# Masked softmax in one pass: 16 pieces of 64 bytes of the output are written early, GpSimd shares the lengths and fills later

## The chip, the cores and the metric

One core of one Trainium2 chip. Times are microseconds (us) of device time for one execution. The spans in the profile are some 2 us shorter than these times (155.5 against 157.49 in the same execution). Where a run was timed in rounds, "ratio" is the mean time of one kernel's fast runs over the mean of the other kernel's fast runs of the same rounds, so it is not quite the ratio of the medians quoted. Single times are used here only for differences of a microsecond or more.

## The reference

`x` is 16 x 8 x 256 x 256 fp32, and `lengths` gives one length between 128 and 255 for each batch.

```python
result = np.zeros_like(x)
for b in range(batch):
    length = lengths[b]
    masked = x[b, :, :, :length].copy()
    masked = masked - np.max(masked, axis=-1, keepdims=True)
    exp_masked = np.exp(masked)
    result[b, :, :, :length] = exp_masked / np.sum(exp_masked, axis=-1, keepdims=True)
```

## The kernel before

A batch is 2.1 MB: 128 partitions of 16 rows of 256 numbers, in one of eight slots of SBUF, the core's on-chip memory (HBM is the large memory that holds `x` and the output). SyncE loads the first four batches and issues every store, on one queue. GpSimd loads the other twelve, each only as wide as its length needs, after filling the unread right-hand columns of four slots once with zeros. VectorE masks, ScalarE takes exponentials with row sums, VectorE multiplies by the inverse sums.

```python
for h in range(2):
    s = slice(h * half, (h + 1) * half)
    nc.sync.dma_start(out=xt[:, 0, s], in_=x_f[0, :, s]).then_inc(s_ld[h], 16)
nc.scalar.dma_start(out=word64, in_=lengths[None, :]).then_inc(s_word, 16)
for b in range(1, ahead):                       # ahead = 4
    nc.sync.dma_start(out=xt[:, b], in_=x_f[b]).then_inc(s_ld[b + 1], 16)
for b in range(batch):
    s_b = s_st[b % 2]
    for s in parts(b):                          # halves and quarters of a batch
        nc.sync.wait_ge(s_out, 2 * b + (s.stop - 1) // half + 1)
        if b >= 2 and s.start == 0:
            nc.sync.wait_ge(s_b, 64 * (b // 2 + 1))
        nc.sync.dma_start(out=out_f[b, :, s, :], in_=xt[:, b % slots, s, :]).then_inc(...)
# ... cut ...
nc.gpsimd.dma_start(out=word64_p, in_=lengths[None, :]).then_inc(s_word_p, 16)
# ... two tiny memsets ...
nc.gpsimd.wait_ge(s_v, 1)
for b in range(ahead, slots):
    nc.gpsimd.memset(xt[:, b, :, low:], 0.0).then_inc(s_fill, 1)
nc.gpsimd.wait_ge(s_word_p, 16)
nc.gpsimd.wait_ge(s_fill, slots - ahead)
nc.gpsimd.wait_ge(s_ld[ahead - 1], 16)          # batch 2 has landed
# ... a loop of GpSimd's twelve loads, each with the width its length picks ...

# VectorE: the bounds
nc.vector.wait_ge(s_word, 16)
nc.vector.tensor_copy(out=len_b, in_=word[:, ::2]).then_inc(s_lenb, 1)
nc.vector.wait_ge(s_lenf, 1)                    # TensorE spreads them over the partitions
step(nc.vector.tensor_scalar(out=len_s, in0=len_f, scalar1=big, scalar2=None, op0=ALU.mult))
```

The softmax here doesn't subtract the row's maximum and nothing guards it: scores larger than these inputs give would overflow.

## Time and profile before

| | before |
|---|---|
| time, median of 3 | 157.06 us (156.95 to 157.23) |
| span of the profile | 155.5 us |
| VectorE, ScalarE, GpSimd busy | 77%, 68%, 12% |
| bytes moved | 62.08 MB (28.51 read from HBM, 33.55 written) |

A profile of a kernel like this is read from the rows of the DMA engines first. If they are full from end to end, the time is bytes over rate (here 62.08 MB at a mean of 399 GB/s, 155.6 us, for a span of 155.5), and the question for any change is whether it alters the bytes, the rate, or the idle ends. The prediction below shows those rows. In the timeline, columns are start, duration, engine, line, operation, "out<-in", count, and in brackets how long the engine stood idle before and what ended that. This is GpSimd at the top of the kernel before:

```profile
1.83 0.64 POOL L146 DMA_DIRECT2D word_p<-in_lengths_dram  x1
2.47 0.12 POOL L148 MEMSET seed<- 1x1 f32 x2
2.54 5.33 POOL L151 MEMSET xt<- 128x1536 f32 x4
```

It is busy from 1.83 to 7.87 without a gap. And the view of waits says how long VectorE stood before its masks for a load (total, times, longest):

```profile
DVE xt L197 <- DMA xt<-in_x_dram: 10.2, 6, 2.4
```

### The profile page before, as it was taken

Reading aid. Unit: us, or ns where it says so; the run is one execution under the profiler, and the core shown is the slowest. Engines: PE = TensorE matmul, PEld = TensorE weight load, DVE = VectorE, ACT = ScalarE, POOL = GpSimd, SP = SyncE. Lnnn points to the kernel's source line nnn. Section 1 sums busy time; section 2 is a strip of 40 time slices with the busy share of each in tenths; the row PEclk is TensorE's granted clock in tenths of the full one; section 3 lists DMA queues with packets and bytes.
Section 4 is the critical chain, followed back from the end, with each engine's and each line's share of the span. In section 5 each row is a group of like instructions: output and inputs, shape, how many; then the busy total and the mean of one; then the engine's idle time right before and its main releaser. Section 6 shows DMA issues by size and latency. Waiting matters only on the chain.

```text
span 155.5 us, 1320 instructions
## 1 busy us (share of the span) xinstructions
PE 0.2 (0%) x1; PEld 0.1 (0%) x1; DVE 120.0 (77%) x84; ACT 105.1 (68%) x514; POOL 19.4 (12%) x26
## 2 busy tenths in 40 slices
PE   0000000000000000000000000000000000000000
PEld 0000000000000000000000000000000000000000
DVE  4963999999999968939895999997977999920000
ACT  3029599999989893956969298989592989400000
POOL 7900031003020202002020202020100000000000
DMA  4999999999999999999999999999999999999991
GB/s 116 428 443 426 434 312 388 416 442 427 393 395 410 415 416 406 420 410 413 409 412 419 402 417 406 415 411 405 425 421 432 420 419 432 457 426 422 415 434 61
DMA packets 10452, 62.08 MB, mean 399 GB/s; under 512 B 930, under 2 KB 1026, under 8 KB 7122
## 3 DMA queue, kind: packets, MB, share of 16 engines
q1 hardware_dynamic: 6336, 41.95, 65.9%
q0 software_dynamic: 4112, 20.12, 32.0%
q14 instruction: 2, 0.02, 0.0%
q10 hardware_dynamic: 2, 0.00, 0.0%
HBM read 28.51 MB, written 33.55 MB: 399 GB/s over the span
## 4 chain that ended last, share of the span: by engine, by line
DMA 67%; DVE 11%; issue 6%; POOLq 2%; SPq 1%; POOL 0%; DVEq 0%
DMA xt<-in_x_dram 60%; DVE xt L224 7%; DMA out_dram<-xt 7%; DVE xt L197 3%; POOLq L100 1%; POOLq L136 1%; POOLq L131 1%; SPq L109 1%; DVE inv_sum L221 0%; POOL xt L131 0%; SPq L112 0%; POOLq L159 0%; POOLq L155 0%; DVEq L214 0%; POOLq L161 0%
## 5 line engine op out<-in xcount | busy, mean ns | idle before, releaser
L251 ACT ACTIVATE xt<-xt x256 | 102.4, 402 | 27.2 <-DVE xt L197 27.2
L224 DVE TENSOR_TENSOR xt<-xt,inv_sum 128x2048 f32<-128x2048 f32 x32 | 73.3, 2292 | 1.1
L251 ACT ACTIVATION_READ_ACCUMULATOR xt<-xt x256 | 48.2, 188 | 0.0
L197 DVE SCALAR_TENSOR_TENSOR xt<-down,len_s,xt 128x2048 f32<-128x2048 f32 (+1 forms) x17 | 37.7, 2222 | 11.1 <-DMA xt<-in_x_dram 10.2
L131 POOL DMA_DIRECT2D xt<-in_x_dram x12 | 12.7, 1057 | 89.7 <-issue 45.7
L221 DVE RECIPROCAL inv_sum<-row_sum 128x8 f32<-128x8 f32 x32 | 6.2, 195 | 2.4 <-ACT xt L251 2.4
L185 DVE CAST len_b<-word 1x16 bf16<-1x16 int32 x1 | 5.6, 5595 | 0.4 <-DMA word<-in_lengths_dram 0.4
L151 POOL MEMSET xt<- 128x1536 f32 x4 | 5.3, 1392 | 0.0
L243 ACT ACT_TABLE_LOAD x1 | 1.3, 1283 | 1.6 <-SPq L79 1.6
L180 DVE TENSOR_SCALAR down<-iota_i 128x256 f32<-128x256 int32 x1 | 0.3, 295 | 1.6 <-POOL iota_i L142 1.6
L146 POOL DMA_DIRECT2D word_p<-in_lengths_dram x1 | 0.6, 643 | 0.1
L188 DVE TENSOR_SCALAR len_s<-len_f 128x16 f32<-128x16 f32 x1 | 0.2, 174 | 0.4 <-PE len_f L167 0.4
L142 POOL IOTA iota_i<- 128x256 int32 x1 | 0.3, 331 | 0.6 <-SPq L79 0.6
L243 ACT ACTIVATE warm<-const-float32-0.0 128x1 f32<-128x1 f32 x1 | 0.2, 203 | 0.0
L145 POOL MEMSET ones<- 1x128 bf16 x1 | 0.2, 194 | 0.0
L167 PE MATMUL len_f<-len_b,ones 1*128 1x16 bf16 x1 | 0.2, 168 | 8.0 <-DVE len_b L185 8.0
L269 POOL MEMSET const-float32-0.0<- 128x1 f32 x1 | 0.1, 98 | 0.3 <-issue 0.3
L148 POOL MEMSET seed<- 1x1 f32 x2 | 0.1, 88 | 0.0
L167 PEld LDWEIGHTS len_f<-len_b,ones 1*128 1x128 bf16 x1 | 0.1, 98 | 8.0 <-issue 8.0
L269 POOL MEMSET const-float32-1.0<- 128x1 f32 x1 | 0.1, 98 | 0.0
L269 POOL MEMSET const-bfloat16-1.0<- 128x1 bf16 x1 | 0.1, 98 | 0.0
L269 POOL MEMSET const-uint8-127<- 128x1 uint8 x1 | 0.1, 98 | 0.0
(1 smaller groups left out, 0.0 us busy)
## 6 DMA issues: line engine op xcount, KB each, us to landing
out_dram<-xt SPq DMA_DIRECT2D x16, 1024.0 KB
out_dram<-xt SPq DMA_DIRECT2D x20, 512.0 KB
xt<-in_x_dram SPq DMA_DIRECT2D x3, 2048.0 KB, 16.0
out_dram<-xt SPq DMA_DIRECT2D x3, 2048.0 KB
xt<-in_x_dram POOLq DMA_DIRECT2D x3, 1728.0 KB, 15.9
xt<-in_x_dram POOLq DMA_DIRECT2D x2, 2048.0 KB, 16.0
xt<-in_x_dram POOLq DMA_DIRECT2D x2, 1600.0 KB, 14.5
xt<-in_x_dram POOLq DMA_DIRECT2D x2, 1280.0 KB, 13.6
```

Source lines behind the costliest of these rows:

```text
L100: return nc.values_load(at, engines=[engine], skip_runtime_bounds_check_because="compared with constants, never an address",)
L109: nc.sync.dma_start(out=xt[:, 0, s], in_=x_f[0, :, s]).then_inc(s_ld[h], 16)
L131: nc.gpsimd.dma_start(out=xt[:, slot, :, :w], in_=x_n[:, n, :, :w]).then_inc(s_sw[par], 16)
L136: with nc.gpsimd.If(v <= ws[m]):
L146: nc.gpsimd.dma_start(out=word64_p, in_=lengths[None, :]).then_inc(s_word_p, 16)
L151: nc.gpsimd.memset(xt[:, b, :, low:], 0.0).then_inc(s_fill, 1)
L185: nc.vector.tensor_copy(out=len_b, in_=word[:, ::2]).then_inc(s_lenb, 1)
L197: return nc.vector.scalar_tensor_tensor(out=t, in0=down[:, None, lo:hi].to_broadcast([P, s.stop - s.start, hi - lo]), scalar=len_s[:, b : ...
L221: step(nc.vector.reciprocal(out=inv_sum[:, b, s], in_=row_sum[:, b, s]))
L224: nc.vector.tensor_tensor(out=t, in0=t, in1=inv_sum[:, b, s, None].to_broadcast([P, half, seq_k]), op=ALU.mult,).then_inc(s_out, 1)
L243: nc.scalar.activation(out=warm, in_=nc.const_aps.tensor(0.0, (P, 1), F32), func=EXP)
L251: ins = nc.scalar.activation(out=e, in_=e, func=EXP, accum_out=sum_h[:, bass.ds(i, 1), j])
```

## The change

Two intents. First, the rate falls for some microseconds where the first store comes; if that is an engine's first write to the output, 16 pieces of 64 bytes, meant as one for each engine, written at the top might pay for it early (the true values are stored over them later). Second, VectorE's small cast takes 5.59 us beside GpSimd's early work and ends at 7.89, just after the last of its four fills (7.87; 1.39 each), so GpSimd drops its own copy of the lengths and fills only once the bounds exist.

```diff
-    word64_p = pool.tile([1, batch], mybir.dt.int64, name="word64_p")
-    word_p = word64_p.bitcast(I32)
+    few = 16
+    touch = pool.tile([few, few], F32, name="touch")
@@ before the loads
+        nc.scalar.dma_start(out=word64, in_=lengths[None, :]).then_inc(s_word, 16)
+        out_e = out_f[0].rearrange("(e r) t k -> e r t k", e=few)[:, 0, 0, :few]
+        nc.vector.memset(touch, 0.0).then_inc(s_zero, 1)
+        nc.scalar.wait_ge(s_zero, 1)
+        nc.scalar.dma_start(out=out_e, in_=touch).then_inc(s_touch, 16)
@@ ahead of the stores
+        nc.sync.wait_ge(s_touch, 16)
@@ GpSimd
-        nc.gpsimd.dma_start(out=word64_p, in_=lengths[None, :]).then_inc(s_word_p, 16)
-        nc.gpsimd.wait_ge(s_v, 1)
+        nc.gpsimd.wait_ge(s_v, 2)
...
-        nc.gpsimd.wait_ge(s_word_p, 16)
+        nc.gpsimd.wait_ge(s_word, 16)
...
-                v_len = length(POOL, word_p[0:1, bass.ds(2 * n, 1)])
+                v_len = length(POOL, word[0:1, bass.ds(2 * n, 1)])
```

(The declarations of the semaphores and the line of the lengths in its old place are cut.)

More of the change, by code (lines that the diff above doesn't have):

```diff
@@ L81 @@
         s_word = sem("s_word")
-        s_word_p = sem("s_word_p")
         s_ones = sem("s_ones")
+        s_touch = sem("s_touch")
+        s_zero = sem("s_zero")
         s_lenb = sem("s_lenb")
@@ L109 @@
             nc.sync.dma_start(out=xt[:, 0, s], in_=x_f[0, :, s]).then_inc(s_ld[h], 16)
-        nc.scalar.dma_start(out=word64, in_=lengths[None, :]).then_inc(s_word, 16)
         for b in range(1, ahead):
             nc.sync.dma_start(out=xt[:, b], in_=x_f[b]).then_inc(s_ld[b + 1], 16)
+        nc.sync.wait_ge(s_touch, 16)
         for b in range(batch):
```

## The prediction

> **What bounds the kernel now.** I read the page's busy table and slices first. VectorE is busy 77% of the 155.5 us span and ScalarE 68%, but the row of the DMA engines is full from the second slice to the last but one. In the slices below, each cell is 155.5/40 = 3.9 us; the first row is the mean busy share of the 16 DMA engines in tenths, the second what they moved.
>
> ```profile
> DMA  4999999999999999999999999999999999999991
> GB/s 116 428 443 426 434 312 388 416 442 427 393 395 410 415 416 406 420 410 413 409 412 419 402 417 406 415 411 405 425 421 432 420 419 432 457 426 422 415 434 61
> DMA packets 10452, 62.08 MB, mean 399 GB/s; under 512 B 930, under 2 KB 1026, under 8 KB 7122
> ```
>
> The reader is to see three things: the engines never rest, the bytes are fixed (62.08 MB), and one slice in the middle of full busyness is slow: the sixth, 312 GB/s, with 388 after it. So I cut the span at the stages that the timeline showed (loads of the first four batches alone; the odd stretch; loads and stores mixed; stores alone) in the table of windows. Its last two columns are the DMA share and GB/s.
>
> ```profile
> 1.50:4.00 2.50, 0.00 (x0) 0.00 (x0) 1.99 (x2) 1.49 (x2) 2.40 (x7) 1.00 0.70 197
> 4.00:20.50 16.50, 0.17 (x1) 0.10 (x1) 12.81 (x9) 7.78 (x39) 3.87 (x3) 1.00 1.01 431
> 20.50:24.00 3.50, 0.00 (x0) 0.00 (x0) 3.47 (x4) 3.50 (x19) 1.71 (x2) 1.00 0.97 283
> 24.00:26.00 2.00, 0.00 (x0) 0.00 (x0) 2.00 (x1) 2.00 (x12) 0.03 (x1) 1.00 0.99 412
> 26.00:47.50 21.50, 0.00 (x0) 0.00 (x0) 21.30 (x17) 21.04 (x107) 2.33 (x2) 1.00 1.02 415
> 47.50:123.70 76.20, 0.00 (x0) 0.00 (x0) 65.33 (x48) 59.65 (x295) 8.61 (x8) 1.00 1.02 414
> 123.70:152.30 28.60, 0.00 (x0) 0.00 (x0) 13.15 (x10) 9.64 (x48) 0.00 (x0) 1.00 1.00 426
> ```
>
> Loads alone run at 431, stores alone at 426, the mixture at 414. Only two stretches fall short: the first 2.5 us, and 20.5 to 24, where the share is 0.97 and yet only 283 GB/s move: the packets themselves are slow. At the rate of stores alone the loss is (426 - 283) x 3.5 = 0.50 MB, over 426 GB/s = **1.17 us**. The DMA view of 20.5 to 22.5 says whose packets these are:
>
> ```profile
> DMA packets 32, 0.52 MB, mean 262 GB/s; under 512 B 0, under 2 KB 0, under 8 KB 0
> q1 hardware_dynamic: 32, 0.52, 105.3%
> ```
>
> 32 packets of 16 KB, two per engine, at 1.053 x 2.0 us x 16 / 32 = 1.05 us each, where 16 KB at 431/16 GB/s take 0.61. All lie in the queue of SyncE. By bytes they are the last loads but one: the four batches are 8.39 MB, 7.60 had gone by 20.5 (371 GB/s in the view of that window) and 8.12 by 22.5, which leaves one packet per engine. The first store, issued at 16.73, stands directly behind them in the same queue. The stall thus straddles the turn from reading x to the first writing of the output.
>
> The chain of waits agrees that transfers carry the end: 60% of it is "DMA xt<-in_x_dram", 7% stores, 11% VectorE. Last, the first 10 us of VectorE:
>
> ```profile
> 1.61 0.29 DVE L180 TENSOR_SCALAR down<-iota_i 128x256 f32<-128x256 int32 x1 [1.61 <-POOL iota_i L142]
> 2.30 5.59 DVE L185 CAST len_b<-word 1x16 bf16<-1x16 int32 x1 [0.40 <-DMA word<-in_lengths_dram]
> 8.25 0.17 DVE L188 TENSOR_SCALAR len_s<-len_f 128x16 f32<-128x16 f32 x1 [0.35 <-PE len_f L167]
> 9.29 1.29 DVE L197 SCALAR_TENSOR_TENSOR xt<-down,len_s,xt 128x1024 f32<-128x1024 f32 x1 [0.87 <-DVE len_s L188]
> ```
>
> A cast of 16 numbers takes 5.59 us. On GpSimd a DMA issue (1.83 to 2.47), two small memsets and the four fills (2.54 to 7.87) run without a gap, and the cast ends at 7.89, just as they do. The first mask, and so all compute, starts 9.29 though the first half batch landed at about 1.13 + 5.1 = 6.2 (issue, and shortest time to landing of the loads).
>
> [...]
>
> **The change part by part.** *The touch.* Adds a VectorE memset of 16x16 (beside an idle engine), one ScalarE issue of about 0.5 us (its issue of the lengths took 0.52) and 16 writes of 64 bytes[...]. SyncE's new wait comes before the first store and is satisfied by about 5 us (estimate: issue ends near 2.2, and a first half-batch landing needs some 5), long before any store is ready. ScalarE's table load (1.28 us at 1.64) slips by perhaps 0.5 and is needed only after 7. Direct cost on the end: 0. Intended gain: the 1.17 us above, if the stall is an engine's first write to this output and can be paid early.
> Is it a first time of the engine rather than of an address? The second batch's store is issued at 26.1 to a region 2 MB on, and 26 to 30 shows 414 GB/s, no stall. So a touch of other bytes can plausibly warm the engine.
> But early is not free: the touch arrives near 2.2 us, as the loads do (first packets at 2.1). If the stall blocks the engine, it holds the loads up there by the same time, unless it overlaps their own slow start (197 GB/s).
> *GpSimd's own copy of the lengths goes.* One issue of 0.64 us and 32 small packets (queue 0 shows 32 before 20.5) leave; 32 come with the touch. Nothing on the path: GpSimd's first load waits for batch 2, landed 18.52, in both kernels.
> *Fills after the bounds.* Cast about 0.2 instead of 5.59, so the bounds at about 3.0 instead of 8.42; fills then run 3.0 to 8.4 (4 x 1.39 with their overlap, 5.33), far ahead of 18.52. First mask limited by its load, about 6.3 instead of 9.29: compute starts **3.0 us** earlier. But the stores it frees stand behind loads that end near 23.5 either way, and from there the DMA engines have work to the end. Worth to the end: 0 to 0.2 us (there is one later slow microsecond, 40 to 41).
>
> **The rivals.**
> 1. The stall is prepaid and hidden: 157.06 - 1.2 = 155.9. For it: location and that it happens once. Against: it falls on load packets, not on store packets. Chance 0.45.
> 2. The stall moves to the top and is hidden only partly: about 156.5. Chance 0.25.
> 3. The stall isn't the first write but something else at that moment, above all GpSimd's first large load, issued 20.71 to 21.91. For it: the very time. Against: the later issues of 1.15 us at 36.24 and 42.90 have 434 and 394 GB/s beside them, and its packets start only near 26. Then 157.0[...]. Chance 0.3.
> 4. The earlier compute is worth its whole 3.0 us, about 154. Only if VectorE set the pace; with full DMA rows I give it little.
>
> **Range and chances.** 0.45 x 1.2 + 0.25 x 0.6 + 0 = 0.69, so 157.06 - 0.7 = **156.4 us**. Low end: full gain, the 0.2 and a bit of the start, 155.5. High end: no gain and a small new hitch, 157.3. Faster by over 2% needs 153.9, which only the fourth rival reaches: 0.03. Slower by over 2% needs 160.2, a new wait that I can't see: 0.03. Within 2%: 0.94.
>
> **What would show it.** Right: a cast of a few tenths; first mask near 6.3; fills beside it without lengthening it; no slice near 20 us below 400 GB/s, and no wait by SyncE on the touch. The second rival shows the first slices poorer by some 0.3 to 0.5 MB; the third shows the dip unchanged. The prediction is wrong if the mixed stage changes its rate of 414: one per cent there is 1 us, as much as the whole stall.

(0.45 x 1.2 + 0.25 x 0.6 = 0.69 us, which from 157.06 gives the 156.4, a ratio of 0.9955. "Two per engine" and "one packet per engine" are means over the 16 engines, as no view gives packets by engine. That the stores stand behind the loads can be seen in the trace: of SyncE's queue the last load packet starts at 23.17 us, the first packet of the store issued at 16.73 at 23.43.)

## The result, and the profile after

Timed on one chip, the changed kernel took 156.94 us (median of 4; 156.77 to 157.30) and the kernel before 157.14 (156.95 to 157.36): ratio 0.999, 95% interval 0.9968 to 1.0012. Timed again in five rounds on another occasion, the ratio was 1.0011 (0.9989 to 1.0032). The change is worth nothing that can be seen. The forecast of 0.7 us, ratio 0.9955, lies below both intervals.

The slices of the changed kernel (busy share in tenths, GB/s; 155.0/40 = 3.9 us each):

```profile
DMA  4999999999999999999999999999999999999993
GB/s 112 421 452 419 444 309 374 417 429 435 403 409 396 411 413 407 429 407 411 410 413 420 404 419 403 408 412 412 425 405 449 420 419 429 440 435 435 416 419 129
DMA packets 10452, 62.08 MB, mean 400 GB/s; under 512 B 930, under 2 KB 1026, under 8 KB 7122
```

The sixth slice is as poor as it was (309 GB/s against 312), and the bytes and packets are the same: 32 small packets left GpSimd's queue and 32 came with the touch. In windows of equal bounds (last two columns: DMA share, GB/s; packets count in the window in which they start, so a share can pass 1), before:

```profile
4.00:20.00 16.00, 0.17 (x1) 0.10 (x1) 12.31 (x9) 7.28 (x36) 3.87 (x3) 1.00 1.02 433
20.00:24.00 4.00, 0.00 (x0) 0.00 (x0) 3.97 (x4) 4.00 (x22) 1.71 (x2) 1.00 0.96 293
24.00:28.00 4.00, 0.00 (x0) 0.00 (x0) 3.97 (x3) 4.00 (x22) 0.03 (x1) 1.00 0.99 410
```

and after:

```profile
4.00:20.00 16.00, 0.00 (x0) 0.00 (x0) 10.92 (x8) 9.94 (x49) 4.40 (x4) 1.00 1.02 433
20.00:24.00 4.00, 0.00 (x0) 0.00 (x0) 3.93 (x5) 4.00 (x21) 1.29 (x1) 1.00 0.92 281
24.00:28.00 4.00, 0.00 (x0) 0.00 (x0) 4.00 (x2) 4.00 (x21) 0.56 (x1) 1.00 1.00 411
```

The stall stands where it stood. In it the packets are slow: SyncE's 32 packets of 16 KB from 20.5 to 22.5 us took a mean of 1.05 us before and 1.01 after, where those from 8 to 20 us took 0.61 in both. The touch itself, by the timeline of the changed kernel and by its DMA view of 5 to 7 us:

```profile
1.67 0.36 ACTq L114 DMA_DIRECT2D out_dram<-touch  x1
```

```profile
q1 hardware_dynamic: 118, 0.84, 99.0%
q10 hardware_dynamic: 32, 0.00, 1.0%
```

Its 32 packets (queue q10 is ScalarE's; 16 packets of 64 bytes and 16 of 4 by the trace's records) ran at 5 to 7 us, not near 2; beside them queue q1 kept 0.84 MB in 2 us, 420 GB/s. So the touch was late, harmless and useless (the run sp_touch below shows that an early one is just as useless).

The second half of the change did just what it should. The timeline of the changed kernel, first 10 us:

```profile
2.33 0.16 DVE L192 CAST len_b<-word 1x16 bf16<-1x16 int32 x1 [0.42 <-DMA word<-in_lengths_dram]
...
2.84 0.17 DVE L195 TENSOR_SCALAR len_s<-len_f 128x16 f32<-128x16 f32 x1 [0.35 <-PE len_f L174]
3.07 5.33 POOL L158 MEMSET xt<- 128x1536 f32 x4 [1.13 <-DVE len_s L195]
...
6.59 1.28 DVE L204 SCALAR_TENSOR_TENSOR xt<-down,len_s,xt 128x1024 f32<-128x1024 f32 x1 [3.58 <-DMA xt<-in_x_dram]
```

The cast takes 0.16 us where it took 5.59. The first mask starts at 6.59 instead of 9.29, waits for its load and nothing else, and takes 1.28 us beside the fills against 1.29 without them. The first store is issued at 14.10 instead of 16.73. None of this reaches the end. The waits of the changed kernel say where the lead went:

```profile
DVE xt L204 <- DMA xt<-in_x_dram: 18.2, 10, 3.6
```

VectorE, 2.7 us ahead at its first mask, waits 8.0 us more than before (3.6 of it ahead of that mask) for loads that the full DMA engines bring no sooner.

### The profile page after: what moved, and what is told of

Read it like the earlier page. It is cut to its first block, busy times and chain, and to the rows that moved or that the text cites. A ratio compares the mean times of both kernels' runs of the same rounds, so it can differ in the third digit from the quotient of the medians.

```text
span 155.0 us, 1322 instructions
## 1 busy us (share of the span) xinstructions
PE 0.2 (0%) x1; PEld 0.1 (0%) x1; DVE 115.1 (74%) x85; ACT 105.2 (68%) x514; POOL 19.0 (12%) x25
## 4 chain that ended last, share of the span: by engine, by line
DMA 66%; DVE 15%; issue 5%; POOLq 2%; SPq 1%; DVEq 0%
DMA xt<-in_x_dram 58%; DVE xt L231 10%; DMA out_dram<-xt 8%; DVE xt L204 5%; DVE inv_sum L228 1%; SPq L117 1%; POOLq L144 0%; POOLq L139 0%; POOLq L101 0%; SPq L119 0%; SPq L127 0%; DVEq L221 0%; POOLq L166 0%; POOLq L162 0%; POOLq L168 0%
## 5 line engine op out<-in xcount | busy, mean ns | idle before, releaser
L192 DVE CAST len_b<-word 1x16 bf16<-1x16 int32 x1 | 0.2, 163 | 0.4 <-DMA word<-in_lengths_dram 0.4
```

## The experiments

The theory was that an engine's first write to the output stalls; its rivals were that the stall is merely moved, or that it belongs to GpSimd's first large load. Every kernel below gave the right result. All edits are to the changed kernel unless said otherwise. One measure serves throughout: the rate in two windows, 4 to 20 us ("top", the loads) and 20 to 28 us ("turn", where stores begin). Against 433 GB/s (top of the kernel before) and 417 (the changed kernel from 28 to 47.5), a shortfall times the window's length gives the megabytes lost. For the kernel before the turn loses (417 - 352) x 8 = 0.52 MB.

| kernel | us | top GB/s | turn GB/s | lost at top, MB | lost at turn, MB |
|---|---|---|---|---|---|
| before | 157.14 | 433 | 352 | 0.00 | 0.52 |
| changed | 156.94 | 433 | 346 | 0.00 | 0.57 |
| store_early | 157.06 | 403 | 415 | 0.48 | 0.02 |
| wide_touch, 128 x 64 B | 156.80 | 429 | 361 | 0.06 | 0.45 |
| few_4k, 16 x 4 KB | 157.01 | 432 | 353 | 0.02 | 0.51 |
| one_row, 1 x 16 KB | 156.57 | 432 | 355 | 0.02 | 0.50 |
| wide_1k, 128 x 1 KB | 157.96 | 423 | 379 | 0.16 | 0.30 |
| big_touch, 128 x 8 KB | 159.25 | 407 | 426 | 0.42 | -0.07 |
| big_far, 128 x 8 KB elsewhere | 159.30 | 413 | 417 | 0.32 | 0.00 |
| sbuf_copy, SBUF to SBUF, 128 x 8 KB | 159.50 | 414 | 422 | 0.30 | -0.04 |
| hbm_copy, HBM to HBM, 128 x 8 KB | 159.34 | 432 | 359 | 0.02 | 0.46 |

(Single times where no rounds are named. In store_early the first store itself falls in the top window. Some 0.05 to 0.1 MB of these figures is the grain of the windows: a packet of 16 KB counts where it starts.)

### Where does the stall belong: to the stores or to GpSimd's first load?

**hold_store**: the first store waits until batch 3 has landed.

```diff
         nc.sync.wait_ge(s_touch, 16)
+        nc.sync.wait_ge(s_ld[ahead], 16)
```

> The first store is issued only once batch 3 has landed (about 24.2 us) instead of at 14.1. T-turn (the stall belongs to the turn from loads to the first stores, which are queued behind them): the packets of SyncE's loads between 20.5 and 22.5 take 0.61 us each as before 20.5 (about 410 GB/s or more until the loads end), and a slow stretch shows after the store's issue instead. T-pool (the stall is GpSimd's first large DMA issue at 20.85): still under 300 GB/s from 20.5 to 24. The time itself may be 1 to 2 us longer, as there is a gap in the supply of work.

Measured: one run of 157.56 us against 156.76 of the kernel before. The windows (DMA share, GB/s last):

```profile
20.00:22.00 2.00, 0.00 (x0) 0.00 (x0) 1.97 (x3) 2.00 (x12) 1.20 (x1) 1.00 1.01 434
...
25.00:28.00 3.00, 0.00 (x0) 0.00 (x0) 3.00 (x2) 3.00 (x16) 0.00 (x0) 1.00 1.00 281
```

SyncE's loads now run to their end at 434 GB/s although GpSimd issues its load at 20.80, in the midst of them: with no store behind them they are not held up. From 22 to 24 us the supply is short (161 GB/s). After the first store's issue at 23.59 comes a slow stretch. There the packets are GpSimd's loads (157 of 168, by the DMA view), which slow to 281 GB/s in total while the store's own packets appear only after 27. It looks as if the turn to stores holds up whatever else an engine has in hand, but pool_late, next, shows GpSimd's loads as slow with no first store about, so this stretch alone does not prove it.

**pool_late** and **pool_early** move GpSimd's first load instead.

```diff
-        nc.gpsimd.wait_ge(s_ld[ahead - 1], 16)
+        nc.gpsimd.wait_ge(s_ld[ahead], 16)     # pool_late
+        nc.gpsimd.wait_ge(s_ld[1], 16)         # pool_early
```

> GpSimd's first load waits for batch 3 (about 24) instead of batch 2 (18.5), so it is issued near 26. T-pool: 20.5 to 24 at over 400 GB/s, and a slow stretch of about 1.2 us of loss at 26 to 28. T-turn: still under 300 GB/s from 20.5 to 24, none at 26. Time within 1 us of the changed kernel in both.

> GpSimd's first load waits for the second half of batch 0 (about 8.9 us) and is issued near 11. T-pool: a slow stretch at about 11 to 13.5 (under 300 GB/s) and none where the loads of SyncE end. T-turn: full rate at 11 to 13.5, and the slow stretch again just ahead of the first store's packets, wherever these come now (later than 20.5, as two streams of loads share the engines).

Measured, pool_late (GpSimd's issue at 27.15):

```profile
20.00:24.00 4.00, 0.00 (x0) 0.00 (x0) 3.93 (x5) 4.00 (x22) 0.00 (x0) 1.00 0.95 303
26.00:30.00 4.00, 0.00 (x0) 0.00 (x0) 3.96 (x3) 4.00 (x22) 1.29 (x1) 1.00 1.02 421
48.00:51.50 3.50, 0.00 (x0) 0.00 (x0) 3.50 (x2) 3.20 (x17) 1.15 (x1) 1.00 1.03 300
```

The stall stays, and none comes with GpSimd's issue. Its one time was 158.20, a microsecond or so longer, more than I had expected. The trace says where: at 48 to 51.5 us, where the queue of stores has run dry and nearly all the bytes are GpSimd's loads (0.96 of 1.05 MB), only 300 GB/s move, which loses (417 - 300) x 3.5 = 0.41 MB. So in this run a second stall, of the size of the first, came after more than 20 us of stores. It began before the next store's issue (49.36), and no run here shows its cause. In pool_early (issue at 11.48) 11 to 14 us had 426 GB/s; the slow stretch came later, at 24 to 26.5, with 345 GB/s, and the run took 156.85. GpSimd's first load is cleared of the stall near 20 us.

**store_early**: the first half store goes ahead of batch 3's load.

```diff
-        for b in range(1, ahead):
+        for b in range(1, ahead - 1):
             nc.sync.dma_start(out=xt[:, b], in_=x_f[b]).then_inc(s_ld[b + 1], 16)
         nc.sync.wait_ge(s_touch, 16)
+        nc.sync.wait_ge(s_out, 1)
+        nc.sync.dma_start(out=out_f[0, :, :half, :], in_=xt[:, 0, :half, :]).then_inc(s_st[0], 32)
+        b = ahead - 1
+        nc.sync.dma_start(out=xt[:, b], in_=x_f[b]).then_inc(s_ld[b + 1], 16)
         for b in range(batch):
             s_b = s_st[b % 2]
-            for s in parts(b):
+            for s in parts(b)[(b == 0) :]:      # the half already stored is skipped
```

> SyncE issues batch 0's first half store at about 14.1 us ahead of batch 3's load, so the first store's packets come after batch 2's load, near 17.5. T-turn: the slow stretch (some 1.2 us of loss) moves to about 15.5 to 19 and 20.5 to 23 is over 400 GB/s. T-pool: it stays at about 20.5 to 24, with GpSimd's issue near 20.8. Time within 1 us of the changed kernel.

Measured, 157.06 us:

```profile
15.50:19.00 3.50, 0.00 (x0) 0.00 (x0) 3.23 (x3) 2.43 (x13) 0.00 (x0) 1.00 0.95 297
20.00:24.00 4.00, 0.00 (x0) 0.00 (x0) 3.97 (x3) 4.00 (x21) 1.30 (x1) 1.00 1.07 444
```

The stall moved with the store. Thus it belongs to the first store, as the prediction held. At the second turn from loads to stores, 24 to 28 us, 385 GB/s were left; against 417 that is 0.13 MB, a quarter of the first, and over 20 to 28 us together 0.02. It is in the main a thing of the first time.

### Then why does the touch not prepay it?

**sp_touch** (the touch issued by SyncE ahead of its loads) and **wide_touch** (the regions of all 128 partitions, in place of 16):

```diff
-        nc.scalar.wait_ge(s_zero, 1)
-        nc.scalar.dma_start(out=out_e, in_=touch).then_inc(s_touch, 16)
+        nc.sync.wait_ge(s_zero, 1)             # sp_touch
+        nc.sync.dma_start(out=out_e, in_=touch).then_inc(s_touch, 16)
```
```diff
-    touch = pool.tile([few, few], F32, name="touch")
+    touch = pool.tile([P, few], F32, name="touch")      # wide_touch
-        out_e = out_f[0].rearrange("(e r) t k -> e r t k", e=few)[:, 0, 0, :few]
+        out_e = out_f[0][:, 0, :few]
```

> The same 16 pieces of 64 bytes, but issued by SyncE ahead of its loads, so that the first write of SyncE's own queue is at the top. If the stall is the first write of that queue, 20 to 24 us goes to over 400 GB/s and the first 4 us lose up to 0.5 MB. If it is not a matter of the queue, 20 to 24 stays under 300 GB/s.

> The touch writes 64 bytes at the start of all 128 partitions' regions of batch 0 (128 pieces[...]) in place of 16[...]. If the stall belongs to addresses that the 16 pieces missed, 20 to 24 us goes from under 300 to over 400 GB/s. If it belongs to the queue of SyncE, or to the volume of writing, or to the kind of packet, the stretch stays under 310 GB/s.

("8 KB per engine" under wide_1k is a mean: 131 KB over 16 engines.)

Measured: sp_touch 157.44 us with a turn of 356 GB/s; its loads are issued 0.6 us later (1.74 instead of 1.13). Its touch ran at 2 to 2.5 us (32 small packets by the DMA view), ahead of every load, so lateness isn't what makes the touch useless either. Its 20 to 24 us had 322 GB/s where I had expected under 300; the later loads may push the stall later, and the turn as a whole is as poor as before. wide_touch 156.80 with a turn of 361. Neither the queue nor the missed regions explain the failure.

**big_touch** writes 1.05 MB of zeros, **big_far** writes them to the last batch's region, 31 MB away.

```diff
-    touch = pool.tile([few, few], F32, name="touch")
+    touch = pool.tile([P, nt // 2, seq_k], F32, name="touch")
-        out_e = out_f[0].rearrange("(e r) t k -> e r t k", e=few)[:, 0, 0, :few]
+        out_e = out_f[0][:, : nt // 2, :]               # big_touch
+        out_e = out_f[batch - 1][:, : nt // 2, :]       # big_far
```

> The touch writes the whole first half of batch 0 (128 x 8 KB of zeros, 1.05 MB, from the queue of ScalarE, stored over later) at the top. It adds 2.5 us of bytes. If volume or addresses are what the small touch lacked, the stall shows at the top (some 1 us of extra loss within the first 10 us) and 20 to 26 us is over 400 GB/s up to the end of the loads and past it. If the stall belongs to the queue of SyncE, a stretch under 310 GB/s shows again ahead of that queue's first store, some 2.5 us later than in the changed kernel.

> The 1.05 MB touch again, but of the last batch's region, 31 MB away from what is stored first. If the engines' path to the output is what has to be opened, as with the near one: a stall of about 0.4 MB within 5 to 9 us, none ahead of the first store (every microsecond from 20 to 27 over 380 GB/s), about 159.2 us. If it is a matter of addresses: stall at the top and a second one ahead of the first store, near 23 to 26 us, about 160.2 us.

Measured: both clear the turn (426 and 417 GB/s), and both lose it at the top (0.42 and 0.32 MB). So the stall can be prepaid, the address in the output doesn't matter, and the times, 2.0 to 2.5 us longer than the kernel before of their rounds for 1.05 MB more (2.5 us at 426 GB/s), show no clear saving.

**wide_1k**, **few_4k** and **one_row** look for the dose.

```diff
+    touch = pool.tile([P, seq_k], F32, name="touch")            # wide_1k
+        out_e = out_f[0][:, 0, :]
+    touch = pool.tile([few, 4 * seq_k], F32, name="touch")      # few_4k
+        out_e = out_f[0].rearrange("(e r) t k -> e r (t k)", e=few)[:, 0, : 4 * seq_k]
+    touch = pool.tile([1, nt * seq_k], F32, name="touch")       # one_row
+        out_e = out_f[0].rearrange("p t k -> p (t k)")[0:1, :]
```

> 128 pieces of 1 KB (131 KB) in place of 16 of 64 bytes. If volume counts and 8 KB per engine is enough, the stall is at the top (some 0.4 MB lost within 3 to 9 us) and 20 to 24 us is over 400 GB/s, time within 0.5 us of the changed kernel's, as it is moved and not hidden. If 8 KB per engine is too little, 20 to 24 stays under 310.

> 16 pieces of 4 KB[...] (65 KB). Between the small touch and the one of 128 x 8 KB: if a packet of full size is what counts, 20 to 24 us is over 400 GB/s and the stall is at the top; if the volume per engine counts, it is in part (300 to 400) or not at all (under 300) prepaid.

> One partition's 16 KB[...]. If the stall is paid per engine, 20 to 24 us stays under 310 GB/s. If it is paid once for all engines together, 20 to 24 is over 400, and if then the other 15 engines are not held up at the top, this is the version that gains, by up to 1.1 us: about 155.9.

Measured: 128 pieces of 1 KB prepay part of it (0.16 MB lost at the top, 0.30 at the turn, together 0.46). 16 pieces of 4 KB and one packet of 16 KB prepay nothing. In each row of the table the two losses add up to 0.26 to 0.57 MB: the debt is paid once, wherever. The three rows with nothing left at the turn and 1.05 MB more (big_touch, big_far, sbuf_copy) have the smallest sums, 0.26 to 0.35. Paying early may thus be cheaper by some 0.2 MB, 0.5 us at 426 GB/s (an estimate); single times, which spread over 0.9 us for one kernel, can neither show nor exclude it. The single 156.57 us of one_row is inside the spread of the kernel before (156.47 to 157.41 in eleven runs) and its turn is as slow as ever, so I make nothing of it.

### Can it hide in the loads' own slow start, and what is it?

**early_1k** and **early_8k** copy x to the output at once, as ScalarE's very first instruction, so that no memset has to come first.

```diff
+        nc.scalar.dma_start(out=out_f[0][:, :1, :], in_=x_f[0][:, :1, :]).then_inc(s_touch, 16)   # early_8k: :8
         nc.scalar.dma_start(out=word64, in_=lengths[None, :]).then_inc(s_word, 16)
-        (the touch: its tile, memset, wait and DMA)
```

> In place of the touch, ScalarE's first instruction copies 128 x 1 KB of x straight to the output (wrong values, stored over later), so that the first writes need no memset and come beside the first loads. If its part of the stall (about half, by the run with 128 x 1 KB) hides in the slow start: 20 to 24 us near 350 GB/s, 1.5 to 4 us no poorer than 185, ratio 0.997 to 1.000. If it does not hide: the first 9 us lose another 0.2 MB, ratio 1.001 to 1.005.

> The same with 128 x 8 KB: 2.1 MB more to read and write counted by both sides, 1.05 MB written. If the stall hides in the slow start: 2.5 us for the bytes less 1.0, so about 158.5 us, no loss ahead of the first store. If it is only moved: 159.2 us or more, with 0.4 MB lost within the first 9 us beyond the kernel before.

Measured: the copies' packets still came only at 5 us and later, so the question of hiding was not put to the test, and it stays open. early_1k: ratio 1.0035 (0.9996 to 1.0073), turn 365 GB/s. early_8k held the surprise: 159.28 us, **nothing lost at the top (433 GB/s) and the stall in full at the turn** (358), although 1.05 MB of the output had been written. Writing the output does not prepay the stall. What big_touch and big_far did, and a copy within HBM does not, is read SBUF. But early_8k also delayed the lengths (the cast ran at 10.97), so two cleaner runs followed: **hbm_copy**, the same copy after the lengths, and **sbuf_copy**, from one SBUF tile to an unused one.

```diff
+        nc.scalar.dma_start(out=out_f[0][:, : nt // 2, :], in_=x_f[0][:, : nt // 2, :]).then_inc(s_touch, 16)  # hbm_copy
-        (the touch: its tile, memset, wait and DMA)
```
```diff
+    touch = pool.tile([P, nt // 2, seq_k], F32, name="touch")      # sbuf_copy
+    aside = pool.tile([P, nt // 2, seq_k], F32, name="aside")
-        out_e = ...
-        nc.scalar.dma_start(out=out_e, in_=touch).then_inc(s_touch, 16)
+        nc.scalar.dma_start(out=aside, in_=touch).then_inc(s_touch, 16)
```

> In place of the touch 1.05 MB is copied from x to the output within HBM (stored over later), after the lengths, so compute is on time. T-write (the stall is the first writing of the output in volume): lost at the top, none ahead of the first store. T-read (the stall is the DMA engines' first reading of SBUF): no extra loss in the first 12 us, and about 0.4 MB lost ahead of the first store, near 22.5 to 26.5 us, with windows of 1 us under 300 GB/s.

> In place of the touch 1.05 MB is copied from one SBUF tile to another, unused one, so that nothing of the output is written early. T-read: about 0.4 MB lost at 5 to 9 us and every microsecond from 20 to 27 over 370 GB/s. T-write: no loss at the top, and the slow stretch with windows under 300 GB/s ahead of the first store, near 22.5 to 26.5.

Measured, hbm_copy:

```profile
5.00:8.00 3.00, 0.00 (x0) 0.00 (x0) 1.28 (x1) 0.00 (x0) 3.00 (x3) 1.00 1.01 429
4.00:20.00 16.00, 0.00 (x0) 0.00 (x0) 8.47 (x7) 7.54 (x37) 4.41 (x4) 1.00 1.02 432
20.00:23.00 3.00, 0.00 (x0) 0.00 (x0) 2.89 (x2) 3.00 (x16) 0.00 (x0) 1.00 1.04 431
23.00:27.00 4.00, 0.00 (x0) 0.00 (x0) 3.93 (x5) 4.00 (x22) 1.86 (x2) 1.00 0.90 289
```

and sbuf_copy:

```profile
5.00:8.00 3.00, 0.00 (x0) 0.00 (x0) 1.28 (x1) 0.44 (x2) 3.00 (x3) 1.00 1.01 336
4.00:20.00 16.00, 0.00 (x0) 0.00 (x0) 8.15 (x8) 8.53 (x37) 5.33 (x4) 1.00 1.02 414
20.00:23.00 3.00, 0.00 (x0) 0.00 (x0) 2.90 (x2) 3.00 (x16) 0.00 (x0) 1.00 1.01 431
23.00:27.00 4.00, 0.00 (x0) 0.00 (x0) 3.93 (x5) 4.00 (x21) 1.67 (x2) 1.00 0.96 410
```

Both move 1.05 MB more at the top. After the copy within HBM the stall is there in full, 289 GB/s; after the copy within SBUF it is gone, 410, and its price, 19 GB/s over 16 us or 0.3 MB against the kernel before, is paid at the top. The window from 5 to 8 us shows it at its place: 440 GB/s in the kernel before, 429 and 418 with the copies within HBM (hbm_copy, early_8k), 336, 317 and 298 where SBUF is read (sbuf_copy, big_far, big_touch). There too the slow packets are loads in hand: of 132 packets from 5 to 7.8 us in sbuf_copy one is the copy's. The tile that it reads is not one that the stores read, so the address in SBUF doesn't matter either. (To the letter my expectation for sbuf_copy, every microsecond over 370, was missed: 21 to 22 and 24 to 25 had 328 each, beside neighbours of 475 to 492, which I put down to the grain of 16 KB packets; big_far misses its 380 in the same way, with 344 twice.) The stall is the DMA engines' **first reading of SBUF in volume**, not their first writing of the output: three runs that read SBUF clear the turn, the two that read HBM alone leave it as it was. And of these five, which all add 1.05 MB, the three that prepay (159.25, 159.30, 159.50) are not seen to be faster than the two that don't (159.28, 159.34).

### Are the two halves of the change worth anything alone?

**no_touch** is the changed kernel without the touch, **touch_only** the kernel before with it, **after_again** the changed kernel unaltered.

```diff
-        out_e = ... ; the memset, the wait and the DMA of the touch        # no_touch
-        nc.sync.wait_ge(s_touch, 16)
```
```diff
+        the same lines, added to the kernel before                         # touch_only
```

> The changed kernel without the touch: only the shared lengths and the later fills. All theories that call the touch useless: the same as the changed kernel, 20 to 24 us at 270 to 295 GB/s, time 156.8 to 157.1, ratio to the kernel before 0.998 to 1.001. If the touch costs what it saves elsewhere, this one is faster by 0.3 to 1 us.

> The kernel before with the small touch alone (GpSimd's own lengths and its early fills stay). If the touch is worth nothing: ratio 0.998 to 1.002, 20 to 24 us at 270 to 300 GB/s, first mask at 9.3 us as before. If the touch pays: ratio near 0.993.

> The changed kernel unaltered. If the change is worth nothing: ratio 0.998 to 1.001 with an interval that holds 1. If the touch or the earlier compute pays what I forecast: ratio near 0.9955 with an interval below 0.998.

Measured: no_touch 0.9988 (0.9949 to 1.0026), turn 352 GB/s; touch_only 1.0017 (0.9999 to 1.0036), turn 357 (20 to 24 us 307, just above the 300 I had expected), its first mask at 9.30 as before; after_again 1.0011 (0.9989 to 1.0032). All hold 1, if touch_only only just: it may cost a tenth or two of a percent.

## Why the prediction was right or wrong

**The time** of 156.94 lies in the stated range, but for the wrong reason: the centre rested on a gain of 0.7 us that did not come.

**The step that failed** is the intended gain: "the 1.17 us above, if the stall is an engine's first write to this output and can be paid early". The place and the size of the stall were right (0.5 MB, once, at the first store; hold_store, pool_late, store_early). The cause was not. It is the first bulk reading of SBUF (hbm_copy against sbuf_copy). Only the third rival, "something else at that moment", left room for that, and it named GpSimd's load, because I described the first store by its target and never by its source. In place of a gain of 1.17 us the runs showed none: the stall stood, 281 GB/s at 20 to 24 us against 293 before, and the ratio was 0.999. The supporting argument, that a later region shows no stall and so any bytes can warm an engine, was half right: addresses don't matter (big_far), but volume does. With 128 partitions, 8 KB in all left 0.45 MB at the turn, 131 KB 0.30, 1.05 MB nothing; the touch reads 1 KB in all.

**The terms of the sum.** 0.45 x 1.2 for a hidden prepayment: measured zero. 0.25 x 0.6 for a partly hidden one: zero too, as the touch moved nothing; even with enough volume no gain is seen (the five runs of 159.25 to 159.50). The first rival should have been given less and the second should have allowed for "moves, and gains nothing": that sentence stood in the text ("it holds the loads up there by the same time"), but I weighed it too lightly.

**The third rival** was right that the first write is not it, and its sign, the dip unchanged, is what came. The thing that it named, GpSimd's first load, is refuted by pool_late and pool_early. Its number, 157.0, came out because the touch does nothing. (Two of the readings beside it are a little off and change nothing: 26 to 30 us had 410 GB/s, not 414, and 434 and 394 are rates of 2 us about the later issues; while they ran it was 395 and 388.)

**The touch "arrives near 2.2 us", satisfied "by about 5"**: wrong. It ran at 5 to 7 us (first packet at 5.5, 3.9 us after its issue at 1.67) and landed 5.3 us after the issue. SyncE's first load, issued at 1.13, had its first packets at 2.2, and from 2 to 5 us all packets but two of the lengths are the loads' (108 of 110). The estimate had allowed for some 5 us to landing, but put the touch among the first packets; why it came only after so many of the loads' is not shown.

**The cast, the fills, the masks**: right. 0.16 us for "about 0.2", bounds at 3.0, first mask at 6.59 for "about 6.3", no lengthening beside the fills (1.28 against 1.29; no run had shown that before). The lead was worth nothing at the end, as its term (0 to 0.2) said; it turned into 8.0 us more of waiting for loads. The fourth rival is refuted by the same line, and by no_touch.

**What stays open**: what in the engines or their path makes the first bulk reading of SBUF slow, where exactly between 64 KB from 16 partitions (nothing prepaid), 131 KB from 128 (part) and 1.05 MB from 128 (all) it is paid, whether the volume or the number of partitions counts between the first two, what the second stall of pool_late is, whether paying early is cheaper by some 0.2 MB, and whether it could be hidden if it came within the loads' own slow start at 2 to 4 us. No version here beats the kernel before by more than the noise.

## What to carry to other kernels

When a transfer stalls the first time, vary its source and its target one at a time before you prepay it: a copy from HBM to HBM and one from SBUF to SBUF told apart in two runs what the touches had not. Where the DMA engines are full, moving a one-time cost of theirs is not yet saving it: here it was moved in three runs, and no time showed a gain; whether it can be put into time when they are idle was not tested. And an engine started 2.7 us earlier bought only longer waits (8.0 us more in all), as the loads it waits for came no sooner.
